# GpSimd takes over the wait for the last store, and ScalarE takes seven eighths of a shared row, in a row-normalising kernel

## The chip, the cores and the metric

The kernel runs on one core of one Trainium2 chip. The metric is the device time of one execution in microseconds (us). A profile is one more execution, recorded instruction by instruction; its span (first to last instruction) is about 1.8 us shorter than the timed figure, because the launch and what follows the program lie outside it.

## The reference

```python
def setup_inputs():
    batch, dim = 1024, 4096          # x: float32; axis -1; eps 1e-12
def reference(x, axis, eps):
    norm = np.sqrt(np.sum(x ** 2, axis=axis, keepdims=True) + eps)
    return (x / norm).astype(np.float32)
```

Each of 1024 rows is divided by its norm. 16.8 MB are read and 16.8 MB written.

## The kernel before

The rows lie four to a partition in two groups of 128 x 4 x 4096, 8.39 MB each. There are four transfers, all on SyncE's queue: load 0, load 1, store 0, store 1. Both loads are issued at once, and a store when its group is scaled. In the traces each transfer is 128 packets of 64 KB on 16 DMA engines, eight to an engine. When an engine's part is done, it adds one to the transfer's semaphore (a counter on which other engines wait); a transfer has landed when all 16 have been counted.

```python
for i, g in enumerate(groups):
    g.square_dve(R - 1); g.square_act(0); g.norm(0); g.scale(0)
    ...                                  # rows 1 and 3 likewise
    g.square_act(2); g.norm(2)
    if i < n_tiles - 1:
        g.scale_by_both(2)               # group 0: the shared row
    else:
        g.scale(2)
    store = nc.sync.dma_start(out=out_t[i], in_=g.flat())
one_barrier_behind_last_store(nc, store.ins)
```

In group 0 the last row is scaled by two engines, the first `cut` columns by ScalarE and the rest by VectorE. Store 0 waits for both.

```python
def scale_by_both(self, r):
    cut = 3 * self.D // 4
    rstd = self.rstd[:, r : r + 1]
    self.nc.scalar.activation(out=self.x[:, r, :cut], in_=self.x[:, r, :cut],
                              func=ACT_F.Copy, scale=rstd)
    self.nc.vector.tensor_scalar_mul(out=self.x[:, r, cut:], in0=self.x[:, r, cut:], scalar1=rstd)
```

The program ends with two barriers. At each, four engines announce their arrival on a semaphore, GpSimd waits for four arrivals and releases them; behind the second, GpSimd clears the semaphores. (A drain, below, is one of the tail's short instructions, on which some of these waits and announcements hang.) `one_barrier_behind_last_store` edits this tail, so that SyncE waits for the last store between the two barriers:

```
SyncE : wait store 1 -> drain -> drain, announce arrival -> wait for release
GpSimd: reset drain -> wait for 4 arrivals -> release -> clear the semaphores
```

## Time and profile before

| | before |
|---|---|
| three runs | 82.28, 82.08, 82.28 us |
| span in the profile | 80.4 us |
| busy: VectorE, ScalarE, the DMA queue | 34%, 36%, 97.1% |

The chain of work that ended last, and the page's list of DMA issues (the last column is the median from issue to landing, in us):

```profile
DMA xt<-in_x_dram 50%; ACT sq_act L33 9%; DVE xt L64 9%; ACT rstd L53 1%; DVE rstd L59 0%
...
xt<-in_x_dram SPq DMA_DIRECT2D x2, 31.2
out_dram<-xt SPq DMA_DIRECT2D x2, 22.8
```

The shares of the chain add up to some 70%. The chain stops at the last scale and leaves out the stores, so it must not be taken for the whole. A store takes 22.8 us from issue to landing although 8.39 MB take only 8 x 2.418 = 19.3 us; most of the rest is time in which it stands behind the transfer ahead of it.

### The profile page before, as it was taken

How to read it: one execution, taken by the hardware profiler on the slowest of the kernel's cores; microseconds unless marked ns; L12 is line 12 of the kernel's file. 1: busy time of each engine (PE TensorE's matmuls, PEld its weight loads, DVE VectorE, ACT ScalarE, POOL GpSimd, SP SyncE). 2: the span in 40 equal slices, each digit the busy share in tenths (PEclk: the TensorE clock that was granted, in tenths of full speed). 3: DMA queues.
4: the chain of work that ended last, by engine and by line, in shares of the span. 5: the costliest groups of instructions: out<-in, count | busy, mean ns of one | idle time of the engine just before them, and what ended most of it. 6: DMA issues, size and time to landing. Idle time of an engine off the chain costs nothing.

```text
span 80.4 us, 94 instructions
## 1 busy us (share of the span) xinstructions
DVE 27.0 (34%) x21; ACT 29.3 (36%) x23; POOL 0.2 (0%) x4
## 2 busy tenths in 40 slices
DVE  0000000000199599970049995999100000000000
ACT  6000000000199999989049999940000000000000
POOL 0000000000000000000000000000000000000000
DMA  9099999399999399999399999499999399999390
GB/s 521 33 489 521 521 521 424 130 489 521 521 521 424 130 489 521 521 521 424 130 489 521 521 489 391 196 489 521 521 489 391 163 521 521 521 489 391 163 521 0
DMA packets 576, 33.55 MB, mean 417 GB/s; under 512 B 64, under 2 KB 64, under 8 KB 64
## 3 DMA queue, kind: packets, MB, share of 16 engines
q1 hardware_dynamic: 576, 33.55, 97.1%
HBM read 16.78 MB, written 16.78 MB: 417 GB/s over the span
## 4 chain that ended last, share of the span: by engine, by line
DMA 50%; ACT 10%; DVE 9%; issue 0%
DMA xt<-in_x_dram 50%; ACT sq_act L33 9%; DVE xt L64 9%; ACT rstd L53 1%; DVE rstd L59 0%
## 5 line engine op out<-in xcount | busy, mean ns | idle before, releaser
L33 ACT ACTIVATE sq_act<-xt 128x4096 f32<-128x4096 f32 x6 | 21.6, 3608 | 22.9 <-DMA xt<-in_x_dram 22.9
L42 DVE SCALAR_TENSOR_TENSOR sq_dve<-xt 128x4096 f32<-128x4096 f32 x2 | 8.9, 4426 | 26.1 <-DMA xt<-in_x_dram 26.1
L64 DVE TENSOR_SCALAR xt<-xt,rstd 128x4096 f32<-128x4096 f32 x7 | 16.5, 2353 | 0.2
L72 ACT ACTIVATE xt<-xt,rstd 128x3072 f32<-128x3072 f32 x1 | 2.9, 2857 | 0.2 <-DVE rstd L59 0.2
L53 ACT ACTIVATE rstd<-ssq,eps_t 128x1 f32<-128x1 f32 x8 | 2.1, 288 | 0.1
L59 DVE RECIPROCAL rstd<-rstd 128x1 f32<-128x1 f32 x8 | 1.3, 159 | 2.4 <-ACT rstd L53 2.4
L33 ACT ACT_TABLE_LOAD x1 | 1.3, 1283 | 0.8 <-PEq L241 0.8
L53 ACT ACT_TABLE_LOAD x1 | 1.3, 1283 | 0.0
L33 ACT ACTIVATION_READ_ACCUMULATOR sq_act<-xt 128x1 f32 x6 | 1.1, 186 | 0.0
L78 DVE TENSOR_SCALAR xt<-xt,rstd 128x1024 f32<-128x1024 f32 x1 | 0.8, 753 | 0.0
L194 DVE MEMSET eps_t<- 128x1 f32 x1 | 0.1, 59 | 0.9 <-PEq L241 0.9
L42 DVE DVE_READ_ACCUMULATOR sq_dve<-xt 128x1 f32 x2 | 0.2, 84 | 0.0
L241 POOL MEMSET const-bfloat16-1.0<- 128x1 bf16 x1 | 0.1, 101 | 0.0
L241 POOL MEMSET const-uint8-127<- 128x1 uint8 x1 | 0.1, 101 | 0.0
L241 POOL MEMSET const-float32-0.0<- 128x1 f32 x1 | 0.1, 98 | 0.2 <-issue 0.2
L241 POOL MEMSET const-float32-1.0<- 128x1 f32 x1 | 0.1, 98 | 0.0
## 6 DMA issues: line engine op xcount, KB each, us to landing
xt<-in_x_dram SPq DMA_DIRECT2D x2, 31.2
out_dram<-xt SPq DMA_DIRECT2D x2, 22.8
```

What stands on the lines that cost most here:

```text
L33: self.nc.scalar.activation(out=sq_a, in_=self.x[:, r], func=ACT_F.Square, accum_out=self.ssq[:, r : r + 1],)
L42: self.nc.vector.scalar_tensor_tensor(out=sq_v, in0=self.x[:, r], scalar=1.0, in1=self.x[:, r], op0=ALU.mult, op1=ALU.mult, accum_out=self ...
L53: self.nc.scalar.activation(out=self.rstd[:, r : r + n], in_=self.ssq[:, r : r + n], func=ACT_F.Sqrt, bias=self.eps_t,)
L59: self.nc.vector.reciprocal(out=self.rstd[:, r : r + n], in_=self.rstd[:, r : r + n])
L64: self.nc.vector.tensor_scalar_mul(out=self.x[:, r], in0=self.x[:, r], scalar1=self.rstd[:, r : r + 1])
L72: self.nc.scalar.activation(out=self.x[:, r, :cut], in_=self.x[:, r, :cut], func=ACT_F.Copy, scale=rstd,)
L78: self.nc.vector.tensor_scalar_mul(out=self.x[:, r, cut:], in0=self.x[:, r, cut:], scalar1=rstd)
L194: nc.vector.memset(eps_t, eps)
L241: nc = _bacc.Bacc("TRN2", target_bir_lowering=False, num_devices=1)
```

## The change

It takes SyncE out of the path between the last landing and the end, and shifts part of the shared row from VectorE to ScalarE.

```diff
-        cut = 3 * self.D // 4
+        cut = 7 * self.D // 8
...
-        everything = take(
-            lambda i: i.engine == SP and any(w.id == sem for w in waits(i))
-        )
-        place([everything], lambda i: i.engine == SP and isinstance(i, mybir.InstDrain))
...
+        landed = [w for w in waits(everything) if w.id == sem]
+        rest = mybir.InstDrain(...,     # SyncE's other waits, without the store's
+                on_wait=[w for w in waits(everything) if w.id != sem], on_update=[]
...
+        both = mybir.InstEventSemaphore(..., engine=POOL,
+                on_wait=waits(arrived) + landed,          # 4 arrivals, and store 1
+                on_update=list(arrived.sync_info.on_update),
+        tail[taking:taking] = [reset, both]
```

More of the change, by code (lines that the diff above doesn't have):

```diff
@@ L109, in first_load_to_front, with gpsimd_waits_for_last_store @@
     nc.at_finalize(move)
-def one_barrier_behind_last_store(nc, store):
+def gpsimd_waits_for_last_store(nc, store):
     SP, POOL = mybir.EngineType.SP, mybir.EngineType.Pool
     def waits(i):
-        return i.sync_info.on_wait if i.sync_info is not None else []
+        return list(i.sync_info.on_wait) if i.sync_info is not None else []
     def move(program):
@@ L128, in move @@
         tail = program.main_func.blocks[-1].instructions
-        def take(which):
-            at = next(n for n, i in enumerate(tail) if which(i))
-            return tail.pop(at)
-        def place(instructions, which):
-            at = max(n for n, i in enumerate(tail) if which(i))
-            tail[at:at] = instructions
-        arrivals = [
-            n
-            for n, i in enumerate(tail)
-            if i.engine == SP and isinstance(i, mybir.InstDrain)
-        ]
-        if any(w.id == sem for w in waits(tail[arrivals[-2]])):
-            return
@@ L145, in move, with where @@
-        everything = take(
-            lambda i: i.engine == SP and any(w.id == sem for w in waits(i))
-        )
-        place([everything], lambda i: i.engine == SP and isinstance(i, mybir.InstDrain))
+        def where(which):
+            return [n for n, i in enumerate(tail) if which(i)]
         def semaphore(i):
             return i.engine == POOL and isinstance(i, mybir.InstEventSemaphore)
-        reset = take(
-            lambda i: i.engine == POOL
-            and isinstance(i, mybir.InstDrain)
-            and i.is_reset_sema
-        )
@@ L157, in move @@
-        arrival = [n for n, i in enumerate(tail) if semaphore(i)][-2]
-        tail.insert(arrival, reset)
-        clear = take(lambda i: i.engine == POOL and isinstance(i, mybir.InstISA))
-        tail.insert(1 + max(n for n, i in enumerate(tail) if semaphore(i)), clear)
+        at = where(lambda i: i.engine == SP and any(w.id == sem for w in waits(i)))
+        everything = tail.pop(at[0])
+        landed = [w for w in waits(everything) if w.id == sem]
+        assert len(at) == 1 and len(landed) == 1
@@ new lines, in move @@
+        assert not everything.sync_info.on_update
+        rest = mybir.InstDrain(
+            name=everything.name,
+            engine=SP,
+            debug=everything.debug,
+            sync_info=mybir.SyncInfo(
+                on_wait=[w for w in waits(everything) if w.id != sem], on_update=[]
+            ),
+        )
+        arrival = where(lambda i: i.engine == SP and isinstance(i, mybir.InstDrain))[-1]
+        tail.insert(arrival, rest)
+        reset = tail.pop(
+            where(
+                lambda i: i.engine == POOL
+                and isinstance(i, mybir.InstDrain)
+                and i.is_reset_sema
+            )[0]
+        )
@@ new lines, in move @@
+        taking = where(semaphore)[-2]
+        arrived = tail.pop(taking)
+        assert len(waits(arrived)) == 1
+        both = mybir.InstEventSemaphore(
+            name=arrived.name,
+            engine=POOL,
+            debug=arrived.debug,
+            sync_info=mybir.SyncInfo(
+                on_wait=waits(arrived) + landed,
+                on_update=list(arrived.sync_info.on_update),
+            ),
+        )
+        tail[taking:taking] = [reset, both]
+        clear = tail.pop(
+            where(lambda i: i.engine == POOL and isinstance(i, mybir.InstISA))[0]
+        )
@@ L162, in one_barrier_behind_last_store @@
+        tail.insert(1 + where(semaphore)[-1], clear)
     nc.at_finalize(move)
@@ L223 @@
         store = nc.sync.dma_start(out=out_t[i], in_=g.flat())
-    one_barrier_behind_last_store(nc, store.ins)
+    gpsimd_waits_for_last_store(nc, store.ins)
 _INS = ['x', 'axis', 'eps']
```

## The prediction

> **What bounds the kernel now.** I read the page first, then the engines' timeline, then the sync engine's own waits, then the instructions of the exit line (L255), and last the trace's single records of semaphores and DMA packets in nanoseconds. The page's first, second and third parts:
>
> ```profile
> span 80.4 us, 94 instructions
> DVE 27.0 (34%) x21; ACT 29.3 (36%) x23; POOL 0.2 (0%) x4
> ...
> DMA  9099999399999399999399999499999399999390
> ...
> q1 hardware_dynamic: 576, 33.55, 97.1%
> ```
>
> Neither compute engine is busy for even 40% of the span, and the one DMA queue is busy for 97.1% of it. The tenths that dip to 3 or 4 are an effect of the way 64 KB packets of 2.4 us fall into 2 us slices, not idle time: the packet records show each of the 16 DMA engines going from one packet to the next within a few nanoseconds. There are 512 packets of 64 KB, so 32 to an engine, and most of them take 2.418 us: 32 x 2.418 = 77.4 us. The first packet starts at 1.01 us, the last ends at 79.68 us. So the kernel is four transfers of 8.39 MB (load 0, load 1, store 0, store 1) laid end to end, and compute has only to deliver each store before the transfer ahead of it runs out. The profile's chain of waits follows load 1 and then the compute of the second group, and it ends at 56.7 us with the last scale; it leaves out the 23.7 us after that (80.4 - 56.7), which are the rest of store 0, store 1 and the exit. Two places are left where the change can touch the end: the moment store 0 is issued, and what follows the landing of store 1.
>
> The timeline around store 0:
>
> ```profile
> 35.47 0.75 DVE L78 TENSOR_SCALAR xt<-xt,rstd 128x1024 f32<-128x1024 f32 x1
> 35.47 2.86 ACT L72 ACTIVATE xt<-xt,rstd 128x3072 f32<-128x3072 f32 x1 [0.23 <-DVE rstd L59]
> 38.35 18.72 SPq L223 DMA_DIRECT2D out_dram<-xt  x2
> 41.37 3.62 ACT L33 ACTIVATE sq_act<-xt 128x4096 f32<-128x4096 f32 x1 [3.05 <-DMA xt<-in_x_dram]
> 41.37 4.43 DVE L42 SCALAR_TENSOR_TENSOR sq_dve<-xt 128x4096 f32<-128x4096 f32 x1 [5.15 <-DMA xt<-in_x_dram]
> ```
>
> The columns are start, length, engine, line, operation. The shared scale starts on both engines at 35.47; VectorE is done 2.1 us before ScalarE, and store 0 is issued at 38.35, as soon as ScalarE has finished. (The 18.72 is two issues merged; the second is at 56.72.) Afterwards both engines idle, ScalarE for 3.05 us and VectorE for 5.15 us, until load 1 has landed. The packet records add what this view does not show: the first packet of store 0 starts at 40.211 us, 2 ns after the last packet of load 1 on the same DMA engine ended. Store 0 thus sat ready behind load 1.
>
> The sync engine's waits and, for the last half microsecond, the exit line's instructions:
>
> ```profile
> SPq L223 <- ACT xt L72: 2.1, 1, 2.1
> ...
> SPq L255 <- DMA out_dram<-xt: 22.5, 2, 19.3
> ```
>
> ```profile
> L255 SPq EVENT_SEMAPHORE  x2: 17/22/28, 80.0 to 80.3; - x2
> L255 SPq DRAIN  x2: 7/7/7, 80.1 to 80.2; - x2
> L255 POOLq EVENT_SEMAPHORE  x2: 17/17/17, 80.2 to 80.3; - x2
> ...
> L255 POOLq EVENT_SEMAPHORE_RANGE_CLEAR  x1: 71/71/71, 80.4 to 80.4; - x1
> ```
>
> After the last landing nothing runs but a relay: SyncE's wait on the store, two drains on SyncE, the second of which announces SyncE's arrival, GpSimd's wait for four arrivals, GpSimd's release, and GpSimd's clearing of the semaphores. Everything else at the second barrier was there long before. In nanoseconds from the span's start, from the trace's records:
>
> ```
> 80031  16th landing of store 1      80047  SyncE: wait on store 1 passes
> 80114  SyncE: drain                 80174  SyncE: drain, announces arrival
> 80183  arrival counted              80207  GpSimd: wait for 4 arrivals passes
> 80285  GpSimd: release              80366  GpSimd: clear (71 ns), span ends 80437
> ```
>
> **What the Trainium skill says.** Four places bear on this.
> - "Perfetto Trace Analysis", section "Sequencer-only Instruction (DRAIN, etc)": the reported start of such an instruction is when all its semaphores are satisfied, and neither its wait nor the spreading of its own update is in the reported length. The trace agrees: the drains are reported at 7 ns each, but they start 60 to 67 ns apart, so the cost of an exit instruction has to be read from start to start.
> - "DMA: Bandwidth & Descriptors", section "Queues, rings and completion order": on each DMA engine descriptors are consumed in ring order. The trace agrees, with the 2 ns between load 1 and store 0.
> - The same page, section "Why a DMA increments its semaphore by 16 and not by 1": each engine posts one count after its data, and only all 16 mean that everything landed. The trace shows 16 landings of store 1 from 79.225 to 80.031 us; the last one alone counts, and it comes 0.27 us after the fifteenth (79.763).
> - "ScalarE: Activation LUTs", section "What ACT_TABLE_LOAD costs": about 280 ns plus 0.833 ns an element for an ACTIVATE with a [128,1] pointer bias. This one has a pointer scale instead, but the trace agrees: 3072 x 0.833 = 2559, and 2857 - 2559 leaves 298.
>
> **The change, part 1: seven eighths.** ScalarE's part grows from 3072 to 3584 columns, 512 more at 0.833 ns = 0.43 us, so about 3.28 us (an estimate from that page and the 2857 ns). VectorE's part falls to 512 columns: its 4096-column scale takes 2353 ns and its 1024-column one 753, so 0.521 ns a column and about 0.49 us, a saving of 0.27 us that nobody waits for. ScalarE was already the later of the two, so the issue of store 0 moves from 38.35 to about 38.78. Does the queue run dry? Load 0 shows 1.01 us from its issue to its first packet on an idle queue. Store 0 could then begin at about 39.79, and the earliest DMA engine is free at 40.21. About 0.4 us of margin stays of the former 0.85. ScalarE ends at about 38.75, 2.6 us before its next work arrives. Direct cost on the end: 0.
>
> **The change, part 2: the exit.** In the built program three things differ. SyncE no longer waits on store 1 at all; its remaining waits and its two drains are over after store 0's landing at 60.7 us, some 19 us early. GpSimd's wait at the second barrier now has two conditions, four arrivals and store 1. The reset drain and the final clear stand where they stood. So from the 16th landing to GpSimd's wait there is one hop in place of wait, drain, drain, hop. Before: 80207 - 80031 = 176 ns. After: GpSimd's reaction to a semaphore, read from its own hop of 24 ns (80183 to 80207), plus 11 ns because SyncE's event with two conditions takes 28 ns where those with one take 17. That is about 25 to 35 ns in all, so 140 to 150 ns are saved. Release, clear and what the runtime does after them follow at the same distances (80437 - 80207 = 230 ns), so the saving reaches the end whole. Sum: 0 - 0.145 = -0.145 us, 0.18% of 82.28.
>
> **The rivals.**
> First, store 0 comes too late and leaves a hole in the queue. Against it stand the 0.4 us of margin. For it: the 1.01 us was measured on an idle queue at the start, and with all 16 engines busy the descriptors might be slower. A hole would be at most some tenths of a microsecond, and every tenth would go straight to the end, because the queue has no idle time to absorb it: 82.1 to 82.6.
>
> Second, the new moment of issue changes a stretched packet. Where store 0 is issued, several of load 1's last packets are longer than 2.418 us: 2.504, 2.466, 2.508, and 2.631 for the one that starts last, at 38.410. That DMA engine is then 0.2 us further behind the others, keeps that lag through both stores, and it is the one that lands last at 80.031. I can't tell from one trace whether the issue causes this. If it does, an issue 0.43 us later may stretch another engine's packet, or none, and the end comes up to 0.2 us earlier; or it may lengthen the last one a little more. The spread of the three times, 82.08 against twice 82.28, is of the same size. This would make 81.9 to 82.3. I lean slightly to a gain, because in the trace the slow packet already sits on the worst engine, and take 0.05 us for it.
>
> Third, GpSimd may be slower than SyncE with a wait on a DMA's semaphore, or two conditions may be checked one after the other with a restart. Nothing in this trace shows GpSimd waiting on a DMA. At the size of a sequencer step here (60 to 80 ns) it would halve the gain: 82.2.
>
> Fourth, the exit is hidden anyway by something after the span. The time is 82.28 and the span 80.44, so 1.84 us lie outside. All engines but GpSimd leave on the release, and GpSimd on its clear, so nothing there can start before the end of this relay. I give this little weight.
>
> **Range and chances.** 82.28 - 0.145 - 0.05 = 82.08 us. The low end takes the whole 0.2 us of the stretched packet as a gain and a little spread: 81.85. The high end takes no gain from the exit and 0.1 us of loss or spread: 82.38. Two per cent is 1.65 us. The exit from landing to end lasts only 0.41 us (80437 - 80031) in all, and the transfers, which are untouched, fill nearly everything else, so a gain of 2% has no source. A loss of 2% would take a hole of 1.65 us ahead of store 0, against an estimated margin. Faster 1%, within 2% 98%, slower 1%.
>
> **What would show it.** In the profile of after: ScalarE's shared scale at 3.2 to 3.3 us and VectorE's near 0.5; the issue of store 0 at 38.7 to 38.8; its first packet still within a few nanoseconds of the end of load 1's; no wait of SyncE on store 1; GpSimd's wait passing 20 to 40 ns after the 16th landing; the same 230 ns from there to the end of the span. The span should then be about 80.3 us or lower. The prediction would be wrong if the queue shows a hole near 40.2 us, if GpSimd takes over 0.1 us to see the landing, or if the last landing itself moves by more than 0.2 us.

## The result, and the profile after

| | runs | median | mean | lowest to highest |
|---|---|---|---|---|
| before | 6 | 82.22 us | 82.20 us | 82.08 to 82.28 |
| after | 6 | 81.92 us | 81.915 us | 81.84 to 81.96 |

The ratio is 0.9965, with a 95% interval from 0.9952 to 0.9978. A ratio is the mean time of one kernel's runs over that of the other's of the same rounds, so it is not quite the ratio of the medians. 0.285 us of gain is clear of the noise.

The page of the changed kernel, in the parts that the prediction showed of before:

```profile
span 80.1 us, 93 instructions
DVE 26.7 (33%) x21; ACT 29.7 (37%) x23; POOL 0.2 (0%) x4
...
DMA  9199996599993899993999993999993999993990
...
q1 hardware_dynamic: 576, 33.55, 97.3%
```

ScalarE gained 0.4 us of work and VectorE lost 0.3; nothing about the kernel's bound has changed, and the span is 0.3 us shorter. The timeline around store 0:

```profile
35.52 3.28 ACT L72 ACTIVATE xt<-xt,rstd 128x3584 f32<-128x3584 f32 x1 [0.23 <-DVE rstd L59]
35.53 0.49 DVE L78 TENSOR_SCALAR xt<-xt,rstd 128x512 f32<-128x512 f32 x1
38.83 0.35 SPq L238 DMA_DIRECT2D out_dram<-xt  x1
41.26 3.62 ACT L33 ACTIVATE sq_act<-xt 128x4096 f32<-128x4096 f32 x1 [2.45 <-DMA xt<-in_x_dram]
41.26 4.43 DVE L42 SCALAR_TENSOR_TENSOR sq_dve<-xt 128x4096 f32<-128x4096 f32 x1 [5.25 <-DMA xt<-in_x_dram]
```

Store 0 is issued 0.48 us later than before, at 38.83. The surprise is in the last two lines: the engines get load 1 at 41.26, while before they got it at 41.37. A store that was issued later went together with a load that landed earlier. The sync engine's waits, then the exit line's instructions from 60.5 us on:

```profile
SPq L270 <- PEq L270: 19.5, 2, 19.3
...
SPq L270 <- DMA out_dram<-xt: 3.2, 1, 3.2
SPq L238 <- ACT xt L72: 2.8, 1, 2.8
```

```profile
L270 SPq DRAIN  x2: 7/7/7, 60.7 to 60.7; - x2
L270 POOLq EVENT_SEMAPHORE  x2: 17/9580/19142, 60.8 to 80.0; - x2
...
L270 POOLq EVENT_SEMAPHORE_RANGE_CLEAR  x1: 71/71/71, 80.0 to 80.0; - x1
```

SyncE waited for store 0 alone (3.2 us) and sent its arrival at 60.7; its 19.3 us are now the wait for the release. GpSimd's wait is recorded with a length of 19,142 ns: its record starts at 60.76 us, when the fourth arrival came, and ends at 79.898, 30 ns after store 1 landed at 79.868. So the time of the second condition lies inside the record.

From the two traces' semaphore and packet records, along the DMA engine that finishes last, the span's 326 ns split as follows. (The trace does not name a packet's DMA engine. An engine is here a chain of packets, each of which starts within 5 ns of the end of the one before; behind a gap, starts and ends are matched in order of time.)

| piece | before, ns | after, ns | difference |
|---|---|---|---|
| to the start of the last packet of load 1 | 38410 | 38470 | +60 |
| that packet, until store 0's first starts | 2633 | 2431 | -202 |
| until store 1's last packet starts | 36222 | 36218 | -4 |
| that packet and its landing | 2766 | 2749 | -17 |
| from the landing to the end of the span | 406 | 243 | -163 |

Two terms matter: the exit, and the hand-over from load 1 to store 0 on each DMA engine.

### The profile page after: what moved, and what is told of

Read it like the earlier page. It is cut to its first block, busy times and chain, and to the rows that moved or that the text cites. A ratio compares the mean times of both kernels' runs of the same rounds, so it can differ in the third digit from the quotient of the medians.

```text
span 80.1 us, 93 instructions
## 1 busy us (share of the span) xinstructions
DVE 26.7 (33%) x21; ACT 29.7 (37%) x23; POOL 0.2 (0%) x4
## 4 chain that ended last, share of the span: by engine, by line
DMA 50%; ACT 10%; DVE 9%; issue 0%
DMA xt<-in_x_dram 50%; ACT sq_act L33 9%; DVE xt L64 9%; ACT rstd L53 1%; DVE rstd L59 0%
## 5 line engine op out<-in xcount | busy, mean ns | idle before, releaser
L72 ACT ACTIVATE xt<-xt,rstd 128x3584 f32<-128x3584 f32 x1 | 3.3, 3282 | 0.2 <-DVE rstd L59 0.2
L78 DVE TENSOR_SCALAR xt<-xt,rstd 128x512 f32<-128x512 f32 x1 | 0.5, 486 | 0.0
```

## The experiments

Theory A: the exit gives 0.16 us in every execution, and the moment at which store 0 is issued costs or saves time at the end of load 1. Theory B: the stretched packet in the trace of before was chance, and the cut does nothing. Twelve runs were made, each timed in five rounds beside the kernel before (`m1_five_eighths` has six times), in three groups on three chips. A kernel's stretches and idle times are read from one profiled execution each. The diffs are against the changed kernel unless said otherwise.

### The two parts alone, and a control

The control is the kernel before without an edit. `a1_exit_only` has

```diff
-        cut = 7 * self.D // 8
+        cut = 3 * self.D // 4
```

and `a2_cut_only` is the kernel before with

```diff
-        cut = 3 * self.D // 4
+        cut = 7 * self.D // 8
```

> The kernel before, unchanged: a control, and a second profile of it. If the stretched packet comes from issuing store 0 at 38.35 us (theory A), this profile again has one packet of 0.1 to 0.25 us over 2.418 us among those running at the issue, and the last landing lags the fifteenth by 0.15 us or more. If it was chance (theory B), the packets are over by 14 ns at most here, and the last landing is within 0.1 us of the fifteenth. Time: 82.1 to 82.3 us either way, ratio 0.999 to 1.001.

> New exit, cut left at three quarters. Both theories: 230 to 255 ns from the last landing to the end of the span instead of 406, so 0.15 to 0.18 us off the time. Theory A (the moment of the issue costs a stretched packet): only that, 82.03 to 82.08 us where before is 82.20. Theory B (the stretched packet is chance and the exit also saves something outside the span): the whole gain of the change, 81.9 to 81.95.

> Cut at seven eighths, exit as before. Theory A: store 0 issued at 38.83, no packet stretched by over 0.05 us, last landing at 79.85 to 79.9, exit still 406 ns; 0.10 to 0.20 us off the time, 82.0 to 82.1 us where before is 82.20. Theory B: no change of the time, ratio 0.9995 to 1.0005.

| run | ratio to before, 95% interval | issue of store 0, us | longest stretch of load 1's last packets, ns | landing to end, ns |
|---|---|---|---|---|
| c0_before_again | 1.0008 (0.9995 to 1.0020) | 38.28 | 354 | 407 |
| a1_exit_only | 0.9988 (0.9975 to 1.0000) | 38.33 | 203 | 243 |
| a2_cut_only | 0.9990 (0.9977 to 1.0002) | 38.72 | 16 | 407 |

"Stretch" is the length of a 64 KB packet over 2418 ns, here of the last packet of load 1 on each of the 16 DMA engines. The times alone don't settle it: the control differs from its twin by 0.07 us, and each half of the change, 0.10 and 0.08 us off the mean, is barely clear of that, with intervals that reach 1.0000 and 1.0002. The profiles do. All three with the cut at three quarters (these two and the first one of before) have stretches of over 0.2 us, and with the cut at seven eighths there are none. The exit goes with its own edit and nothing else. Theory B's forecasts failed for the packets: the stretch came back in the control and left when the cut alone was changed. The distance of the last two landings, which the control's expectation also named as a mark, was 0.23 us in the control and 0.09 in `a2_cut_only`; it carries the spread of the start as well, so the packets are the better mark.

### Issuing store 0 earlier

```diff
-        cut = 7 * self.D // 8
+        cut = 3 * self.D // 8        # f1_early
+        cut = 5 * self.D // 8        # m1_five_eighths
```

At three eighths both engines end together, which looks like the best balance.

> New exit, cut at three eighths, so both engines end together (ScalarE about 1.58 us, VectorE about 1.55 us) and store 0 is issued at about 37.1, 1.3 us earlier than before and some 3.1 us ahead of the first free DMA engine. Theory A: if earlier issues are the harmful ones, packets running at 37.1 are stretched by 0.1 to 0.3 us and the time is 82.03 to 82.15, like the exit alone or worse; Theory B: the same time as the exit alone within 0.05 us. Either way no hole in the queue.

> New exit, cut at five eighths: ScalarE about 2.43 us, store 0 issued at about 37.95, between the 37.21 of the cut at three eighths (last packets of load 1 stretched by 0.5 to 1.1 us) and the 38.33 of three quarters (at most 0.1 to 0.35 us). Theory A, that the loss depends on how long before the end of load 1 store 0 is issued: stretches between the two, 0.2 to 0.6 us on most engines, and 82.15 to 82.5 us where before is 82.15. Theory B, that the slow run at three eighths had another cause (both engines on the shared row, or VectorE's longer part): no stretch and 82.0 us like the exit alone.

`f1_early` took 82.77 us in the mean (ratio 1.0081, 1.0067 to 1.0095), and `m1_five_eighths` 82.43 (1.0039, 1.0025 to 1.0052). The better balanced kernels are the slower ones, and `f1_early` is far worse than expected. Its timeline:

```profile
35.57 1.58 ACT L72 ACTIVATE xt<-xt,rstd 128x1536 f32<-128x1536 f32 x1 [0.23 <-DVE rstd L59]
35.58 1.55 DVE L78 TENSOR_SCALAR xt<-xt,rstd 128x2560 f32<-128x2560 f32 x1
37.21 0.35 SPq L238 DMA_DIRECT2D out_dram<-xt  x1
41.88 3.62 ACT L33 ACTIVATE sq_act<-xt 128x4096 f32<-128x4096 f32 x1 [4.73 <-DMA xt<-in_x_dram]
```

Store 0 goes out 1.6 us earlier than in the changed kernel, and load 1 arrives 0.6 us later, 41.88 against 41.26. My expectation looked for the stretch in the packets running at 37.1. It was in the ones after: all 16 last packets of load 1, which start at 37.9 to 38.5, are 0.5 to 1.1 us too long. The store's own packets take 2.418 us as ever, so nothing is given back.

### The same early split with a late store

ScalarE copies scratch ahead of its part, so that only the moment of the issue moves; `f1_early` is the base:

```diff
         cut = 3 * self.D // 8
         rstd = self.rstd[:, r : r + 1]
+        pad = self.scratch["act"][:, :2245]
+        self.nc.scalar.activation(out=pad, in_=pad, func=ACT_F.Copy)
```

> The changed kernel once more: a second profile, and the mark for the other three. Theory A: no packet at the end of load 1 stretched by over 0.05 us, 235 to 255 ns from last landing to the end, 81.85 to 82.0 us, 0.15 to 0.3 us under before.

> New exit, the cut of three eighths that was 0.6 us slow, but with a copy of 2245 columns of scratch on ScalarE (about 2.05 us) ahead of its part, so that store 0 is issued at about 38.8 as in the changed kernel. Theory A (only the moment of the issue counts): the stretches of 0.5 to 1.1 us are gone and the time is that of the changed kernel within 0.1 us. Theory B (the split itself, VectorE's longer part, made it slow): the time stays at 82.6 to 82.9.

`s1_after_again` took 81.93 us in the mean (ratio 0.9977, 0.9963 to 0.9990), and `k1_early_split_late_store` 81.92 (0.9972, 0.9960 to 0.9985).

```profile
35.25 2.06 ACT L73 ACTIVATE sq_act<-sq_act 128x2245 f32<-128x2245 f32 x1
...
38.80 0.35 SPq L240 DMA_DIRECT2D out_dram<-xt  x1
41.31 4.43 DVE L42 SCALAR_TENSOR_TENSOR sq_dve<-xt 128x4096 f32<-128x4096 f32 x1 [4.18 <-DMA xt<-in_x_dram]
```

Two microseconds of useless work on ScalarE made the slow kernel some 0.85 us faster (82.77 and 81.92, in separate rounds), and as fast as the changed one: its stretches are 14 ns at most. The split is innocent; the moment of the issue is the cause. One thing more is in its packets: the first DMA engine to finish load 1, 1.44 us after the issue, stood idle for 239 ns before its first packet of store 0. The other 15 went on within 3 ns.

### Issuing store 0 later

`d1_all_on_act` gives ScalarE the whole row; `e1_late` has a copy of 960 columns of scratch before that.

```diff
-        cut = 7 * self.D // 8
+        cut = self.D
+        pad = self.scratch["act"][:, :960]                          # e1_late only
+        self.nc.scalar.activation(out=pad, in_=pad, func=ACT_F.Copy)  # e1_late only
-        self.nc.vector.tensor_scalar_mul(out=self.x[:, r, cut:], ...)
```

> New exit, ScalarE does the whole shared row (3.71 us), VectorE none: store 0 issued at about 39.2, 1.0 us before the first DMA engine is free at 40.2. Theory A: no stretched packet, as at seven eighths, and at most a hole of 0.1 us on the earliest engines, while the engine that is free last (40.8) has none: 81.85 to 82.0 us. If the queue needs more than 1.6 us from issue to first packet when it is busy (the rival of the prediction): a hole on all engines and 82.2 or more.

> New exit, all of the shared row on ScalarE, and a copy of 960 columns of scratch before it (about 1.08 us): store 0 issued at about 40.3. If issue to first packet is 1.0 us as at the start, its first packets start at 41.3 instead of 40.2 to 40.9: a hole of 0.4 us behind the last engine, time 82.2 to 82.5 us. If it takes 1.5 us or more: 82.7 or more. This measures the margin that the prediction estimated at 0.4 us.

`d1_all_on_act` took 82.19 us (1.0011, 0.9999 to 1.0023) and `e1_late` 82.27 (1.0019, 1.0006 to 1.0032). Of `d1_all_on_act` first the issue, then `e1_late`:

```profile
39.19 0.35 SPq L235 DMA_DIRECT2D out_dram<-xt  x1
```

```profile
35.17 0.98 ACT L73 ACTIVATE sq_act<-sq_act 128x960 f32<-128x960 f32 x1
35.30 0.16 DVE L59 RECIPROCAL rstd<-rstd 128x1 f32<-128x1 f32 x1 [0.57 <-ACT rstd L53]
36.06 3.69 ACT L74 ACTIVATE xt<-xt,rstd 128x4096 f32<-128x4096 f32 x1
39.78 0.35 SPq L237 DMA_DIRECT2D out_dram<-xt  x1
```

Both expectations missed. In `e1_late` the copy filled ScalarE's wait for VectorE's reciprocal, so that the issue moved to 39.78 only; its time lies in the expected range, but for another moment of issue. And in `d1_all_on_act` there is a hole already: no packet of load 1 is stretched, but 15 DMA engines stand idle for 191 to 243 ns before store 0. As expected, the one that finishes load 1 last, 1.63 us after the issue, has none. In `e1_late` all 16 stand idle, for 194 to 381 ns. From issue to store 0's first packet it is 1.29 us in `d1_all_on_act` but only 0.84 in `e1_late`, so there is no fixed latency that one could subtract. Where an engine does not go straight on, it loses at least some 0.2 us in all these runs; what sets that stays open. In both kernels most packets right after a hand-over are also 28 to 48 ns longer than usual.

All runs in one table. "Lead" is the time from the issue of store 0 to the moment at which the first of load 1's last packets would end after 2418 ns; stretch and hole are of those 16 packets and behind them.

| lead, us | run | mean stretch, ns | largest, ns | hole, ns |
|---|---|---|---|---|
| 3.14 | f1_early | 788 | 1104 | none |
| 2.37 | m1_five_eighths | 328 | 603 | none |
| 1.93, 1.87, 1.85 | c0, a1, the kernel before | 46, 59, 34 | 354, 203, 213 | none |
| 1.53 to 1.33 | s1, a2, k1, h1, after, g1 | 5 to 10 | 16 | none, but 239 on one engine of k1 |
| 1.05 | d1_all_on_act | 1 | 2 | 191 to 243 on 15 engines |
| 0.88 | l1_load_late (below) | 2 | 2 | 189 to 244 |
| 0.46 | e1_late | 1 | 2 | 194 to 381 |

In these runs the best moment is a narrow one, some 1.3 to 1.5 us ahead of the end of the load.

A long lead alone need not do harm. In the same profiles, `l1_load_late` apart, load 1 is issued some 20 us before load 0 ends, and load 0's last packets are at most 4 ns too long. Store 1 is issued 2.8 to 3.4 us before store 0 ends, and store 0's last packets are at most 48 ns too long (none at all in `f1_early`, with 3.2 us). The long stretches were seen only where a store stands behind a load.

### Is load 0's slow start the same effect?

In every profile the first packets of load 0 are longer than 2418 ns too, by 0.54 to 0.81 us in the mean, and load 1 is issued just then, at 0.79 us. `l1_load_late` holds load 1 back behind a chain of copies:

```diff
+        if i == 1:
+            for n in (4096, 4096, 4096, 4096, 2500):
+                nc.scalar.activation(out=sq_act[:, :n], in_=eps_t.to_broadcast([P, n]), func=ACT_F.Copy)
+            nc.scalar.activation(out=g.x[:, 0, :1], in_=sq_act[:, :1], func=ACT_F.Copy)
         load = nc.sync.dma_start(out=g.flat(), in_=x_t[i])
```

> The changed kernel, but load 1 is issued only at about 19.6 us, behind a chain of copies on ScalarE, in place of 0.79 us. The first packets of load 0 take 0.3 to 1.0 us longer than 2.418 in every profile so far. If that comes from the issue of load 1 at 0.79 (theory A carried further: an issue stretches what is in flight), they become 2.42 us and the time falls by 0.5 to 0.7 us, to 81.2 to 81.5. If it belongs to the start of the first load: no change, 81.85 to 82.05 us, or some tenths more if 19.6 is too late.

Load 1 was issued at 19.2 us, and load 0's first packets were as long as ever, 0.76 us over in the mean. So the issue of load 1 does not cause the slow start, and no time is to be had from moving it; the cause stays open. The issue of load 1, 1.7 us ahead of the end of load 0, lengthened load 0's last packets by no more than 14 ns. The run's time (82.26 us, ratio 1.0018) says nothing further: the built program's order on the compute engines moved too, store 0 went out at 39.43, and it had the hole of a late store.

### The exit: two waits, and the release first

`g1_two_waits` puts GpSimd's two conditions on two instructions, with the store's on the reset drain. `h1_release_first` moves the store's wait behind the release; in the built program it ends up on the clear itself.

```diff
-        both = ...                       # the event with two conditions
-        tail[taking:taking] = [reset, both]
+        tail.insert(taking, reset)
+        alone = mybir.InstEventSemaphore(..., engine=POOL, on_wait=landed, on_update=[])
+        tail.insert(taking, alone)                        # g1_two_waits
+        tail.insert(1 + where(semaphore)[-1], alone)      # h1_release_first
```

> The changed kernel with GpSimd's two conditions on two instructions: its reset drain waits for store 1, then its event waits for the four arrivals. If a sequencer step costs 60 to 80 ns as in the relay of before, 60 to 100 ns more from the last landing to the end, 305 to 345 ns instead of 243. If two conditions in one event had cost GpSimd a restart, this is no slower than 243. Time: up to 0.1 us over the changed kernel.

> The changed kernel with the wait on store 1 moved once more, behind GpSimd's release of the barrier onto its last instruction, the clear of the semaphores; the other engines leave some 19 us early. From the last landing to the end about 24 + 71 = 95 to 120 ns instead of 243, so 81.75 to 81.85 us. If what the runtime does afterwards can begin on the engines that left early, up to 0.2 us more than that; if it waits for GpSimd alone, no more.

The exit line's instructions after 79.5 us, of `g1_two_waits` and then of `h1_release_first`:

```profile
L266 POOLq EVENT_SEMAPHORE  x2: 17/17/17, 80.0 to 80.1; - x2
L266 POOLq DRAIN  x1: 64/64/64, 79.9 to 79.9; - x1
...
L266 POOLq EVENT_SEMAPHORE_RANGE_CLEAR  x1: 71/71/71, 80.2 to 80.2; - x1
```

```profile
L266 POOLq EVENT_SEMAPHORE_RANGE_CLEAR  x1: 71/71/71, 79.9 to 79.9; - x1
```

With two waits, 362 ns pass from the landing to the end instead of 243, a little more than expected: the drain (64 ns) stands in the path with its hand-over, and the event passes 108 ns after the drain began. So one event with two conditions was cheaper here than two instructions, by 119 ns. The time was 82.03 us (0.9985, 0.9973 to 0.9998), 0.10 over `s1_after_again`.

With the release first there is one instruction after the landing: 25 ns to its start, 71 ns of clearing, 96 ns in all. That is 147 ns less than in the changed kernel, as expected. The time was 81.75 us in the mean (0.9951, 0.9939 to 0.9964), 0.18 under `s1_after_again` in the same rounds (three of its runs at 81.65 to 81.68, two at 81.83 and 81.90). `h1_release_first` is the best kernel, ahead of both, if by only 0.2%. Its output was correct, but it needs one more assumption: when the other engines leave early, something after the program must still wait for GpSimd. In the trace the runtime does: the update of its semaphore 2 that comes 0.77 us after the landing in the changed kernel comes after 0.62 us here, so it gains those 147 ns and no more.

## Why the prediction was right

The predicted 82.08 us with a range of 81.85 to 82.38 held the measured 81.92, and "within 2%" was right. By its steps:

- **The bound** was read rightly. The transfers are laid end to end, and nearly all of the span's 326 ns came from the hand-over of load 1 to store 0 and from the exit.
- **Part 2, the exit**, was the mechanism that it named: the relay through SyncE is gone, the other waits are over at 60.7, and release and clear follow at the same distances. Its size was 163 ns in place of 140 to 150. The term that was too large is the way from the landing to the release: predicted 25 to 35 ns for GpSimd's reaction and then 78 ns, so 103 to 113 ns, while the release came 92 ns after the landing. The record of GpSimd's wait ends 30 ns after the landing, as forecast, but it runs from before the landing, so how the 92 ns divide can't be read. The third rival (GpSimd slower, or a restart for two conditions) fell, and so did the fourth (the exit hidden by what follows): time less span is 1.84 us in the profiled run before and after.
- **Part 1, the cut**: 3.28 us and 0.49 us came out to the digit, and the issue at 38.83 for 38.78. "Direct cost on the end: 0" holds, as there was no hole. But the margin of "about 0.4 us" behind it was wrong in its making, and the zero was in part luck. It took 1.01 us from issue to first packet, from an idle queue. Engines that finished load 1 as late as 1.54 us after the issue stood idle in `d1_all_on_act`, and one at 1.44 in `k1_early_split_late_store`, while the first of the changed kernel, at 1.41, and of `g1_two_waits`, at 1.33, did not. So no margin can be read from these runs. The first rival, a hole, did not come at seven eighths, but it came with an issue 0.36 us later (`d1_all_on_act`, 82.19 us).
- **The second rival**, the stretched packet, is what happened, and here the size was off. The prediction said "I can't tell from one trace whether the issue causes this", leaned to a gain and took 0.05 us. The last of the 16 hand-overs came 0.16 to 0.25 us later than with packets of 2418 ns in the three profiles at three quarters, and 2 to 16 ns later in the six with leads of 1.33 to 1.53 us. In the timed runs it is less: `a1_exit_only` at 82.03 and the changed kernel at 81.92 and 81.93 differ by 0.11, though in separate rounds.
- **The sum**: of the 0.16 us between 82.08 and 81.92, 0.06 are the start, since before measured 82.22 rather than 82.28 in the larger sample; 0.02 are the exit; the remaining 0.08 are put down to the stretched packet by subtraction, and were not measured alone.

What the DMA engines do while store 0 is early is not shown. The Trainium skill, "DMA: Bandwidth & Descriptors", section "Two DMAs through the same engine are not ordered", says that descriptors start in order but are pipelined, and that an engine's read and write sides have separate queues. That would let a store begin to read beside the end of a load; no run here shows it doing so.

## What to carry to other kernels

Where a store is queued behind a load, look for the best moment of its issue. Here a store issued well ahead of the end of the load lengthened that load, and one issued too late left a hole, so the slower engine of a split can be the right one to load. Behind a transfer of its own kind a long lead did no such harm. At the exit, read start to start what runs after the last landing: the 163 ns cut there came off the span whole. The fastest kernel had a single instruction behind the last wait, provided that what follows still waits for that engine.

## What the Trainium skill lacked or had wrong

- "Perfetto Trace Analysis", section "Sequencer-only Instruction (DRAIN, etc)", says that the reported start is when all semaphores are satisfied, and that the wait is not in the reported length. GpSimd's event with two conditions differs: its record began with the first condition and was 19,142 ns long, the second wait included.
- No page has the effect of a store that is issued early behind a load on the same queue: with a lead of 3.1 us each of the load's last 64 KB packets took 0.5 to 1.1 us longer than 2.418, with 2.4 us 0.15 to 0.6, and with 1.3 to 1.5 us at most 16 ns. Nor has any that a store behind a store showed no more than 48 ns of this, with 2.8 to 3.4 us.
- "DMA: Bandwidth & Descriptors", section "Anatomy of one DMA — SWDGE (gpsimd) path", puts most of a fixed cost of about 2 us on the write receipt, for another path of issue, and that section has no such figure for SyncE's queue. Here the last store's landing came 0.35 us (before) and 0.33 us (after) after its last data packet ended.
- No page says how late a transfer may be issued behind a busy queue: a lead of 1.33 us left no hole, one of 1.44 us a hole of 239 ns on one DMA engine, and one of 1.05 us holes of 191 to 243 ns on 15.
